# A second gate projected in feature layout in a mixed-attention decoder step: new order of the projection, transposes, and additions moved between engines

## The chip, the cores and the metric

The kernel runs on one core of one Trainium2 chip. The metric is the device time of one execution in microseconds; the time before is the median of three runs. A core has five engines that run side by side and each in its own order: TensorE (PE; its weight loads are listed as PEld), VectorE (DVE), ScalarE (ACT), GpSimd (POOL) and SyncE (SP), which here issues the loads.

## The reference

One layer on 512 prompt tokens and 32 sample tokens, model width 1024: a half-step SwiGLU FFN, a mixing layer, a second half-step FFN, a final RMSNorm. The change is in the mixing layer:

```python
h = rmsnorm(x); z = h @ w_in            # columns: q 512 | k 128 | v 128 | u 512 | gv 512
q, k = rope(q), rope(k)
ya = sliding_window_attention(q, k, v, sinks)          # 8 query heads, 2 key heads, window 128
u  = gelu(z_u)
gv = rmsnorm(gelu(z_gv))                               # over the 512 features of a token
yg = u * (tril(W_s) @ gv + b)                          # per chunk of 128 tokens, 8 heads of 64
x  = x + concat(rmsnorm(ya), rmsnorm(yg)) @ w_out
```

All tensors are float32. The prompt's last chunk of gv and the samples' gv are outputs too.

## The kernel before, in words

All 544 tokens are kept in feature layout: 128 features on the partitions, tokens along the row, x as eight such blocks. A GEMM in full precision is split into three fp32r products: the weight tile and the activation are each held as a high part and a low remainder (wh, wl; xh, xl), and high by high, high by low and low by high are added in PSUM. `gemm_T` (L357) goes over k, and for each k issues six matmuls of 272 columns, three products by two halves of the tokens; after each k it calls `tick`. Weights come by DMA as 128x1024 pieces into four raw buffers; ScalarE makes wh of a piece and VectorE wl (`conv`, L306), one step after each piece of the projection (`conv_step`, L332).

The order of instructions on each engine is fixed at build time by a small planner. `Model` (L41) estimates when each engine is free and when each tile is ready, from a cost for every operation. Work is either main line (the GEMMs, written out in order) or side work: generators that yield a list of what they need (a flag, a tile, a free PSUM slot) ahead of each part. `tick` (L175) is called after each k step: if the estimate of VectorE or ScalarE is more than BACKLOG ahead of TensorE's, it places nothing; otherwise it places the first side work whose needs are met (work marked late only when both are below a third of BACKLOG ahead). `force` (L192) places side work without regard to time until a flag is set.

The mixing layer, `mix` (L821), goes through `Z_ORDER` (L32): k, q0, q1, v, q2, u0, u1, q3, then gv in two halves of 256 columns, then u2, u3. A k, q, v or u piece is 128 output features: one `gemm_T` over 8 k, 48 matmuls, into an accumulator (two buffers `acc`, a third `sp` in places). gv is projected in token layout by `z_gv` (L1233) and `tok_gemm` (L1221): for each half, four tiles of 128 tokens and one of 32, each 8 k by three matmuls with the activation as the stationary operand and 256 columns of weights moving. The result is scaled by the token's 1/rms on its way out of PSUM and lies in `gv` (token on the partition, 512 features along the row).

A q piece is rotated on its way out (`ev_z`, L1172): four ScalarE copies, three VectorE passes, then a split into high and low halves (`split_z`, L1193). Side work meanwhile: `outs` (the k and v outputs), eight attention units (`unit`, L905; four query blocks for each of two head pairs jp), the samples (`samples`, L967), the split and row sums of the attention result (`y_gen`, `a_stat`), and `gmlp` (L1116), late work: gelu and norm of gv, then gelu of u and four times `spatial` (L1092), matmuls named mp and msp. A unit makes scores into the PSUM tile sp (needs the split q and k), exponentials on ScalarE into so, transposes so (tp), and multiplies by v (po) into yT.

The output projection (L1283) has two halves, attention first, each 8 blocks m of 24 matmuls named o. For each m, VectorE multiplies the accumulator by the tokens' 1/rms into a buffer (oa, og) and the buffer is added to x: by GpSimd, except for m = 7 of the gated half. In the gated half `post_norm` (L786) follows: ScalarE makes the new xh and squares, VectorE xl and the running sum ss, from which pss_n and the norm of the second FFN come. The first matmuls of that FFN are named agb and aub.

Of the kernel before, what the change touches and what calls it, by code (L numbers as in the profile page):

```python
# [9 lines left out]
ALU = mybir.AluOpType  # L10
PSUM = bass.MemoryType.PSUM

D = 1024
ND = 8
DFF = 2816
NF = 22
NP = 512
NSMP = 32
NT = NP + NSMP
HT = NT // 2  # L20
# [8 lines left out]

Z_ORDER = (("k", 0), ("q", 0), ("q", 1), ("v", 0), ("q", 2), ("u", 0), ("u", 1), ("q", 3),  # L32
           ("g", 0), ("g", 1), ("u", 2), ("u", 3))
RAW_BUFS = 4
W_BUFS = 5
NX = 14
SLACK = 4500.0
BACKLOG = 3500.0


class Model:  # L41


    def __init__(self):
        self.t = dict(PE=0.0, DVE=0.0, ACT=0.0, POOL=0.0, DMA=1500.0)
        self.log = {}
        self.slot = {}
        self.table = None

    def box(self, ap):  # L50
        (ps, pn), *rest = ap.ap
# [10 lines left out]
        return max((e[4] for e in self.log.get(key, ())), default=0.0)  # L62

    def put(self, eng, ns, reads, writes, lat=100.0):
        reads, writes = [self.box(r) for r in reads], [self.box(w) for w in writes]
        t = max([self.t[eng]] + [self.when(r, True, eng) for r in reads] + [self.when(w, False, eng) for w in writes])
        self.t[eng] = t + ns - {"DVE": 85.0, "ACT": 95.0}.get(eng, 0.0)
        for bs, w in ((reads, False), (writes, True)):
            for key, *b in bs:
                old = self.log.get(key, [])  # L70
                if w:
                    old = [e for e in old if not (b[0] <= e[0] and e[1] <= b[1] and b[2] <= e[2] and e[3] <= b[3])]
                self.log[key] = old[-60:] + [(*b, t + ns + lat, w, eng)]
# [66 lines left out]
class Prog:  # L140
# [16 lines left out]
    def ready(self, g, forced=False):  # L157
        t = self.m.t["PE"]
        for n in g[1]:
            if isinstance(n, tuple):  # L160
                if n not in self.flags:
                    return False
            elif callable(n):
                if not n():
                    return False
            elif forced:
                continue
            elif isinstance(n, str):
                if self.m.free(n) > t:
                    return False  # L170
            elif self.m.when(self.m.box(n)) > t:
                return False
        return True

# [270 lines left out]
    @staticmethod  # L445
    def g2(ap):
        return ap.rearrange("p (g n) -> p g n", g=2)
# [373 lines left out]
    def mix(self, pc, hold):  # L821
        nc = self.nc
        tc = self.tc
        a = self.a
        mm = nc.tensor.matmul
        g2 = self.g2
# [3 lines left out]
        with tc.tile_pool(name="mx", bufs=1) as pm, tc.tile_pool(name="mxr", bufs=2) as pr, scratch:  # L830
# [10 lines left out]
            yT = qT  # L841
# [9 lines left out]
            vt = pm.tile([128, 4, 128], F32, name="vt")  # L851
            vs = pm.tile([32, 128], F32, name="vs")
            gv = pm.tile([128, 5, 512], F32, name="gv")
            u = pm.tile([128, 4, NT], F32, name="u")
            ssa = self.p_st.tile([128, NT], F32, tag="ss", bufs=1, name="ssa")

# [22 lines left out]
            S = self.flags  # L879
# [25 lines left out]
            def unit(i, n, jp):  # L905
# [11 lines left out]
                for g in range(2):  # L917
                    for jj in range(2):
                        o = sp[:, g, jj * 256:jj * 256 + w]
# [13 lines left out]
                v = lambda t: t.rearrange("p (g j) -> p g j", g=2)  # L933
# [10 lines left out]
                PT = [t544(f"PT{i}_{kb}")[:, 0:512] for kb in range(nkb)]  # L944
                for kb in range(nkb):
                    if kb:
                        yield ["po"]
                    tp = self.psum(self.p_ms, ("tr", "po")[kb], f"tp{i}_{kb}")
# [3 lines left out]
                S["so", i] = 1  # L952
                if i == len(UNITS) - 1:
                    S["exp",] = 1
                yield [*PT, "tr", ("v", 0), vt]
                po = self.psum(self.p_ms, "tr", f"po{i}")
                for kb in range(nkb):
                    for g in range(2):
# [8 lines left out]
            def samples():  # L967
                qsv = qs.rearrange("p g b j t -> p g b (j t)")
                yield [qs, "sp"]
                t = pr.tile([128, 576], F32, tag="sT", bufs=1, name="sT")  # L970
# [28 lines left out]
                tp = self.psum(self.p_ms, "po", "tps")  # L999
# [4 lines left out]
                nc.vector.tensor_copy(t[0:32, 256:512], tp[0:32, 256:512])  # L1004
                for g in range(2):
                    gs = slice(g * 64, g * 64 + 64)
                    yield [t, "po", vs]
                    po = self.psum(self.p_ms, "po", f"pos{g}")
                    mm(po[gs, 0:128], vs[:, gs], t[0:32, 256 + g * 128:384 + g * 128], start=True, stop=False)
                    for b in range(8):  # L1010
                        mm(po[gs, b * 16:(b + 1) * 16], vc[:, b, gs], t[:, g * 128 + b * 16:g * 128 + (b + 1) * 16],
                           start=False, stop=(b == 7))
                    nc.vector.tensor_copy(yT[gs, :, NP:NT].rearrange("p j (b t) -> p j b t", b=8),
                                          po[gs, 0:128].rearrange("p (b j t) -> p j b t", b=8, j=4))
# [57 lines left out]
            def a_stat(t0, t1):  # L1072
                yield from self.rstat(ssa, 512, "a", hold_a, t0=t0, t1=t1, parts=2)
# [144 lines left out]
                if (kind, j) == ("v", 0):  # L1218
                    self.flush(hold)

            def tok_gemm(out, s, p):  # L1221
                t0, tn = s * 128, (128 if s < 4 else 32)
                for k in range(ND):
                    wh, wl = self.w[p + k // 4]
                    ws = slice((k % 4) * 256, (k % 4) * 256 + 256)
                    oo = out[:tn, 0, 0:256]
                    xh, xl = self.xh[:, k, t0:t0 + tn], self.xl[:, k, t0:t0 + tn]
                    mm(oo, xh, wh[:, ws], start=(k == 0), stop=False)
                    mm(oo, xh, wl[:, ws], start=False, stop=False)
                    mm(oo, xl, wh[:, ws], start=False, stop=(k == ND - 1))  # L1230
                    self.tick()

            def z_gv(gh):  # L1233
                nonlocal pc
                rs = hold["rs"]
                for s in range(5):
                    ac = self.acc(f"zg{gh}{s}")
                    tok_gemm(ac, s, pc)
                    tn, col = (128, rs[:, s:s + 1]) if s < 4 else (32, rs[0:32, 5:6])
                    o = gv[:tn, s, gh * 256:(gh + 1) * 256]  # L1240
                    self.scale(o, ac[:tn, 0, 0:256], col)
                self.conv_step()
                self.conv_step()
                pc += 2
                S["ng"] = S.get("ng", 0) + 1
                if S["ng"] == 2:
                    S["gv",] = 1

            def z_u(j):
                nonlocal pc  # L1250
                ac = self.acc(f"zu{j}")
                self.gemm_T(ac, pc, 0, self.rh, self.rl, range(ND))
                pc += 1
                nc.vector.tensor_tensor(g2(u[:, j, :]), ac[:, :, :HT], g2(hold["R"]), op=ALU.mult)
                self.conv_step()
                S["nu"] = S.get("nu", 0) + 1
                if S["nu"] == 4:
                    S["u",] = 1
# [2 lines left out]
            self.add_side(outs(), ("v",))  # L1261
            self.add_side(a_stat(384, NT), ("nsplit",))
            self.add_side(a_stat(0, 384), ("ys", 0, 0), ("ys", 1, 0))
            self.add_side(samples(), ("q", 3))
            for i, (n, jp) in enumerate(UNITS):
                self.add_side(unit(i, n, jp), ("q", 2 * jp + 1), ("so", i - 2))
# [4 lines left out]
            for kind, j in Z_ORDER:  # L1271
                if kind == "g":
                    self.flush(hold)
                    z_gv(j)
                elif kind == "u":
                    z_u(j)
                else:
                    z_qk(kind, j, S.get("nz", -1) < 2)
# [4 lines left out]
            for half in range(2):  # L1283
                yo = 8 if half == 0 else 4
                for m in range(ND):
# [4 lines left out]
                    if half == 0 and m < 3:  # L1290
# [7 lines left out]
                        ac = early[m]  # L1298
                    else:
                        ac = self.acc(f"o{half}{m}", True)  # L1300
# [11 lines left out]
                    def ev_g(m=m, ac=ac):  # L1312
                        xm = self.x[:, m, :]
                        if m == 0:
                            S["ss2"] = self.p_st.tile([128, NT], F32, tag="ss", bufs=1, name="ss2")
                            S["post"] = self.post_norm(self.cols[:, 16:24], S["ss2"], "n3")
                        t = t544(f"og{m}")
                        nc.vector.tensor_tensor(g2(t), ac[:, :, :HT], g2(hold_g["R"]), op=ALU.mult)
                        (nc.vector if m == 7 else nc.gpsimd).tensor_tensor(xm, xm, t, op=ALU.add)
                        dead(f"og{m}")  # L1320
                        S["post"](m)

# [202 lines left out]
def _arrange(i):  # L1525
# [5 lines left out]
    for l in (1, 2):  # L1531
# [5 lines left out]
        for ci, (f0, nf) in enumerate(CHUNKS[l]):  # L1537
            t = dn[f0:f0 + nf]
# [6 lines left out]
    q, k, v, u, gv = np.split(w, [512, 640, 768, 1280], axis=1)  # L1545
    q = q.reshape(D, 2, 4, 64).transpose(0, 2, 1, 3).reshape(D, 512)
    lay = lambda t, n: t.reshape(ND, 128, n, 2, 128).transpose(2, 1, 3, 0, 4).reshape(n, 128, 2, ND * 128)
    gl = gv.reshape(2, 4, 128, 2, 256).transpose(3, 2, 0, 1, 4).reshape(2, 128, 2, 1024)
    part = dict(k=k, q=q, v=v, u=u)
    rows, pair = [], []  # L1550
    for n, j in Z_ORDER:
        if n == "g":
            rows.append(gl[j:j + 1])
            continue
        pair.append(part[n][:, j * 128:j * 128 + 128])
        if len(pair) == 2:
            rows.append(lay(np.concatenate(pair, axis=1), 1))
            pair = []
# [62 lines left out]
```

## Time and profile before

| | us |
|---|---|
| median of 3 runs | 971.64 (969.87 to 971.93) |
| the profiled execution | 970.15 |
| its span, first to last instruction | 968.4 |
| mean granted TensorE clock | 0.985 of full speed |
| first FFN ends, mixing layer's k piece begins | 383.5 |
| output projection begins | 514.0 |
| last matmul of the output projection | 573.9 |

A profile row of a group or of the timeline gives the operation, its output and its inputs by the program's names, the shapes, and how many; a bracket tells how long the engine stood idle before it and what ended that. The chain of waits is the path followed back from the last instruction; its rows are start, length, what, and how many in a row, so length by count is the spacing of matmuls that keep TensorE busy. The granted clock is the share of full speed that TensorE was given in a stretch. All rows carry L126, the line of the helper through which each instruction is recorded.

### The profile page before, as it was taken

To read this page: it belongs to the slowest core of one execution; us is meant where nothing else is said; L and a number is where in the kernel's file an instruction comes from. 1 tells how busy PE (TensorE), PEld (TensorE's weight loads), DVE (VectorE), ACT (ScalarE), POOL (GpSimd) and SP (SyncE) were. 2 spreads that over 40 slices of the span, in tenths; PEclk is the share of its full clock that TensorE was granted. 3 is DMA by queue.
4 is the path that set the end of the run, shared out by engine and by line. 5 is a ranking of instruction groups with operands and counts; after the bars stand their busy time and mean duration, and the time that the engine had idled before them with its cause. 6 is when DMAs were issued, how large, how long until landed. Compare 5 with 4: busy or idle time off the path is not lost.

```text
span 968.4 us, 18114 instructions
## 1 busy us (share of the span) xinstructions
PE 945.7 (98%) x7491; PEld 934.2 (96%) x7491; DVE 729.9 (75%) x1309; ACT 412.4 (43%) x656; POOL 57.4 (6%) x62
## 2 busy tenths in 40 slices
PE   8999999999999999999999999999999999999996
PEld 8999999999999999988888989999999999999996
DVE  6789996688668957567676694889985799845864
ACT  7434542245234445555574253334442344512432
POOL 0000000000000000030011640000000000000002
PEclk9999999999999999989999998999999999999998
DMA  7421334222422245112121312203242232512202
GB/s 248 132 66 56 106 90 143 88 87 75 144 71 84 74 148 201 62 56 86 49 85 53 97 62 81 94 30 113 89 142 85 73 99 93 173 46 87 81 9 93
DMA packets 29827, 90.88 MB, mean 94 GB/s; under 512 B 3808, under 2 KB 7248, under 8 KB 29600
## 3 DMA queue, kind: packets, MB, share of 16 engines
q1 hardware_dynamic: 28416, 87.85, 27.8%
q0 software_dynamic: 784, 1.30, 0.4%
q8 instruction: 59, 0.97, 0.4%
q10 hardware_dynamic: 544, 0.56, 0.2%
q14 instruction: 24, 0.20, 0.1%
HBM read 86.98 MB, written 3.74 MB: 94 GB/s over the span
## 4 chain that ended last, share of the span: by engine, by line
PE 90%; DVE 4%; ACT 3%; issue 1%; DMA 1%; SPq 0%; POOL 0%; DVEq 0%; ACTq 0%
PE ada L126 14%; PE adb L126 13%; PE o L126 4%; PE aub L126 3%; PE zu L126 3%; PE zg L126 3%; PE agb L126 2%; PE aga L126 2%; PE aua L126 2%; DVE ss L126 1%; PE zq L126 1%; PE pb_40P L126 1%; PE pa_121P L126 1%; PE pa_40P L126 1%; PE pb_161P L126 1%
## 5 line engine op out<-in xcount | busy, mean ns | idle before, releaser
L126 ACT ACTIVATE wh<-raw 128x1024 fp32r<-128x1024 f32 (+2 forms) x240 | 219.7, 940 | 274.1 <-DVE raw L126 154.5
L126 DVE TENSOR_TENSOR wl<-raw,wh 128x1024 fp32r<-128x1024 f32 (+2 forms) x240 | 256.2, 1079 | 12.6 <-ACT wh L126 12.2
L126 PE MATMUL adb<-hhb,wh 128*128 128x272 f32 x352 | 78.5, 289 | 0.7 <-DVE hpb L126 0.7
L126 PE MATMUL adb<-hlb,wh 128*128 128x272 f32 x352 | 78.0, 288 | 0.9 <-DVE hlb L126 0.9
L126 PE MATMUL adb<-hhb,wl 128*128 128x272 f32 x352 | 77.9, 288 | 0.0
L126 DVE TENSOR_TENSOR raw<-raw,raw 128x512 f32<-128x512 f32 x108 | 74.0, 686 | 1.3
L126 PE MATMUL ada<-hha,wh 128*128 128x272 f32 x352 | 72.9, 288 | 0.9 <-ACT wh L126 0.9
L126 PE MATMUL ada<-hla,wh 128*128 128x272 f32 x352 | 72.7, 288 | 0.0
L126 PE MATMUL ada<-hha,wl 128*128 128x272 f32 x352 | 72.6, 287 | 0.0
L126 DVE SCALAR_TENSOR_TENSOR x<-adb,x 128x272 f32<-128x272 f32 x64 | 25.8, 435 | 47.0 <-PE adb L126 46.9
L126 PEld LDWEIGHTS adb<-hlb,wh 128*128 128x128 f32 x352 | 57.3, 188 | 1.2 <-DVE hlb L126 1.2
L126 PEld LDWEIGHTS adb<-hhb,wh 128*128 128x128 f32 x352 | 57.3, 188 | 0.9 <-DVE hpb L126 0.9
L126 DVE SCALAR_TENSOR_TENSOR x<-ada,x 128x272 f32<-128x272 f32 x64 | 25.1, 433 | 42.6 <-PE ada L126 42.6
L126 PEld LDWEIGHTS adb<-hhb,wl 128*128 128x128 f32 x352 | 57.1, 188 | 0.0
L126 PEld LDWEIGHTS ada<-hha,wh 128*128 128x128 f32 x352 | 55.1, 188 | 1.1 <-issue 1.1
L126 PEld LDWEIGHTS ada<-hla,wh 128*128 128x128 f32 x352 | 55.3, 188 | 0.0
L126 PEld LDWEIGHTS ada<-hha,wl 128*128 128x128 f32 x352 | 55.1, 188 | 0.0
L126 ACT ACTIVATE xh<-x,cols 128x544 fp32r<-128x544 f32 x24 | 17.7, 746 | 36.4 <-DVE x L126 18.0
L126 ACT ACTIVATE hhb<-hpb 128x544 fp32r<-128x544 f32 (+1 forms) x24 | 14.8, 621 | 40.0 <-DVE hpb L126 40.0
L126 PE MATMUL o<-xh,wh 128*128 128x272 f32 x128 | 29.3, 295 | 2.2 <-DVE oa L126 2.2
L126 ACT ACTIVATE hha<-hpa 128x544 fp32r<-128x544 f32 x22 | 14.5, 659 | 39.3 <-DVE hpa L126 39.3
L126 PE MATMUL o<-xh,wl 128*128 128x272 f32 x128 | 28.9, 293 | 0.0
(813 smaller groups left out, 2873.9 us busy)
## 6 DMA issues: line engine op xcount, KB each, us to landing
raw<-wgu SPq DMA_DIRECT2D x86, 512.0 KB, 3.9
raw<-wd SPq DMA_DIRECT2D x32, 384.0 KB, 3.3
raw<-wd SPq DMA_DIRECT2D x20, 512.0 KB, 4.6
raw<-win SPq DMA_DIRECT2D x14, 512.0 KB, 4.3
raw<-wout SPq DMA_DIRECT2D x8, 512.0 KB, 3.7
x<-x SPq DMA_DIRECT2D x8, 272.0 KB, 4.9
y<-x SPq DMA_DIRECT2D x6, 272.0 KB, 2.4
raw<-wgu SPq DMA_DIRECT2D x8, 128.0 KB, 3.6
```

The lines of the kernel that those rows point to most:

```text
L126: return f(*args, **kw)
```

## The change

- `Z_ORDER` becomes k, q0, q1, v, g0, q2, g1, q3, g2, g3, u0 to u3. gv is now four pieces of 128 features, each a `gemm_T` like u, and its weights are laid out as the others are.
- A gv piece is copied out unscaled into free rows of other tensors: g0 and g1 into the places of u2 and u3, g2 and g3 into yT's blocks 2 and 3. New side work, `turn_gv`, waits for all four, transposes them on TensorE, four blocks of 128x128 for each token tile, into the PSUM slots po and tr, and scales by 1/rms on the way into `gv`, whose layout stays.
- What overwrites those places waits for the flag gv: the units of jp = 1 and the samples before they write yT, u2 and u3 before they are evicted.
- In the gated half of the output projection all additions to x are VectorE's.
- The planner: BACKLOG 3500 to 2500; a VectorE operation that reads two SBUF operands is taken to start after a GpSimd operation in flight; a margin, set to zero.

```diff
-Z_ORDER = (("k", 0), ("q", 0), ("q", 1), ("v", 0), ("q", 2), ("u", 0), ("u", 1), ("q", 3),
-           ("g", 0), ("g", 1), ("u", 2), ("u", 3))
+Z_ORDER = (("k", 0), ("q", 0), ("q", 1), ("v", 0), ("g", 0), ("q", 2), ("g", 1), ("q", 3), ("g", 2), ("g", 3), ("u", 0), ("u", 1), ("u", 2), ("u", 3))
...
-BACKLOG = 3500.0
+BACKLOG = 2500.0
+MARGIN = 0.0
...
     def put(self, eng, ns, reads, writes, lat=100.0):
+        two = [r for r in reads if len(r.ap) > 1 and r.ap[-1][1] > 1]
...
+        if eng == "DVE" and sum(r.space != PSUM for r in two) == 2 and self.pool[0] <= t < self.pool[1]:
+            t = self.pool[1]
+        if eng == "POOL":
+            self.pool = (t, t + ns)
...
-            elif self.m.when(self.m.box(n)) > t:
+            elif self.m.when(self.m.box(n)) > t - MARGIN:
...
+            gT = lambda j: u[:, 2 + j, :] if j < 2 else yT[:, j, :]
...
-                yield [*PT, "tr", ("v", 0), vt]
+                yield [*PT, "tr", ("v", 0), vt, ("gv",) if jp else ("v", 0)]
...
-                    yield [t, "po", vs]
+                    yield [t, "po", vs, ("gv",)]
...
-            def z_gv(gh):
+            def z_g(j):
                 nonlocal pc
...
+                ac = self.acc(f"zg{j}")
+                self.gemm_T(ac, pc, 0, self.rh, self.rl, range(ND))
+                pc += 1
+                self.scale(g2(gT(j)), ac[:, :, :HT])
+                self.conv_step()
+                S["ng"] = S.get("ng", 0) + 1
+                if S["ng"] == 4:
+                    S["gT",] = 1
+
+            def turn_gv():
+
+                rs = hold["rs"]
                 for s in range(5):
...
+                    t0, tn, col = (s * 128, 128, rs[:, s:s + 1]) if s < 4 else (NP, 32, rs[0:32, 5:6])
+                    slot = ("po", "tr")[s % 2]
+                    yield [*(gT(j)[:, t0:t0 + tn] for j in range(4)), slot]
+                    tp = self.psum(self.p_ms, slot, f"tg{s}")
+                    for j in range(4):
+                        nc.tensor.transpose(tp[:tn, j * 128:(j + 1) * 128], gT(j)[:, t0:t0 + tn], self.ident)
+                    self.scale(gv[:tn, s, :], tp[:tn, :], col)
+                S["gv",] = 1
...
+                if j >= 2:
+                    self.force(lambda: ("gv",) in S)
                 nc.vector.tensor_tensor(g2(u[:, j, :]), ac[:, :, :HT], g2(hold["R"]), op=ALU.mult)
...
+            self.add_side(turn_gv(), ("gT",))
             self.add_side(samples(), ("q", 3))
...
-                        (nc.vector if m == 7 else nc.gpsimd).tensor_tensor(xm, xm, t, op=ALU.add)
+                        nc.vector.tensor_tensor(xm, xm, t, op=ALU.add)
```

More of the change, by code (lines that the diff above doesn't have):

```diff
@@ L48, in __init__ @@
         self.table = None
+        self.pool = (0.0, 0.0)
     def box(self, ap):
@@ L1219, in z_qk @@
                     self.flush(hold)
[L1221 to L1231, printed above, removed]
-            def z_gv(gh):
-                nonlocal pc
+            def z_g(j):
+                nonlocal pc
+                ac = self.acc(f"zg{j}")
[7 more added lines that the diff above has]
+            def turn_gv():
                 rs = hold["rs"]
                 for s in range(5):
[L1237 to L1247, printed above, removed]
+                    t0, tn, col = (s * 128, 128, rs[:, s:s + 1]) if s < 4 else (NP, 32, rs[0:32, 5:6])
[6 more added lines that the diff above has]
+                S["gv",] = 1
             def z_u(j):
@@ L1273, in mix @@
                     self.flush(hold)
-                    z_gv(j)
+                    z_g(j)
                 elif kind == "u":
@@ L1547, in _arrange @@
     lay = lambda t, n: t.reshape(ND, 128, n, 2, 128).transpose(2, 1, 3, 0, 4).reshape(n, 128, 2, ND * 128)
-    gl = gv.reshape(2, 4, 128, 2, 256).transpose(3, 2, 0, 1, 4).reshape(2, 128, 2, 1024)
-    part = dict(k=k, q=q, v=v, u=u)
+    part = dict(k=k, q=q, v=v, u=u, g=gv)
     rows, pair = [], []
     for n, j in Z_ORDER:
-        if n == "g":
-            rows.append(gl[j:j + 1])
-            continue
         pair.append(part[n][:, j * 128:j * 128 + 128])
```

## The prediction

> **What bounds the kernel now.** I read the page first, then who TensorE waited for, then the stretches of the stage between the two FFNs, then the chain of that stage, and last its timeline where TensorE stood still.
>
> The page:
>
> ```profile
> span 968.4 us, 18114 instructions
> PE 945.7 (98%) x7491; PEld 934.2 (96%) x7491; DVE 729.9 (75%) x1309; ACT 412.4 (43%) x656; POOL 57.4 (6%) x62
> ```
>
> TensorE is the bound: 98% busy, VectorE 75%. What can move the time is the number of matmuls, their spacing, and the few places where PE waits. Those places, from the waits of PE over the whole run (line waited for: us in total, times, longest):
>
> ```profile
> PE pss_n L126 <- DVE ss L126: 2.6, 1, 2.6
> PE o L126 <- DVE oa L126: 2.2, 1, 2.2
> PE sp L126 <- DVE xh L126: 1.8, 1, 1.8
> PE zg L126 <- ACT gv L126: 1.1, 1, 1.1
> PE zg L126 <- DVE zc L126: 0.3, 1, 0.3
> PE sp L126 <- DVE xl L126: 0.3, 1, 0.3
> ```
>
> All six lie in the mixing stage, which is what the change edits. The stretches of that stage and of the FFN behind it (length; busy us and instructions of PE, PEld, DVE, ACT, POOL; granted clock; DMA share; GB/s):
>
> ```profile
> 412.00:421.00 9.00, 7.32 (x33) 6.79 (x34) 7.13 (x22) 4.88 (x7) 0.63 (x2) 0.62 0.36 116
> 421.00:450.00 29.00, 29.00 (x233) 27.80 (x233) 16.98 (x55) 17.12 (x44) 8.46 (x17) 1.00 0.19 62
> 450.00:455.00 5.00, 3.60 (x28) 3.23 (x28) 4.21 (x8) 2.77 (x4) 0.00 (x0) 1.00 0.00 0
> 455.00:514.00 59.00, 59.00 (x492) 53.67 (x493) 42.50 (x148) 34.27 (x100) 4.12 (x7) 1.00 0.22 73
> 553.00:581.00 28.00, 25.67 (x205) 25.45 (x204) 26.13 (x27) 14.06 (x20) 12.70 (x8) 1.00 0.23 76
> 581.00:590.00 9.00, 8.73 (x47) 8.73 (x48) 3.88 (x5) 1.35 (x2) 2.10 (x1) 0.62 0.40 132
> 590.00:700.00 110.00, 109.31 (x872) 109.08 (x871) 91.86 (x152) 45.66 (x65) 0.00 (x0) 1.00 0.24 76
> ```
>
> Two things are to be seen. A gap costs more than its idle time: behind the sp gap the clock is 0.62, and 33 matmuls run in 9 us where 421 to 450 has 233 in 29 (8.0 per us); 33 would take 4.1 us, so 4.9 us are lost for 2.1 us of waiting. And behind the stage PE runs without a gap (109.3 of 110 us), so a microsecond that the stage gains reaches the end.
>
> **The change part by part.** The rows that carry the prices, from the chain of waits of the stage (start, us, what):
>
> ```profile
> 424.18 12.03 PE zu L126 x96
> 438.46 0.44 PE tp L126 x4
> 470.60 5.59 PE zg L126 x48
> 484.68 0.58 PE po L126 x4
> 501.56 1.01 PE po L126 x8
> 514.00 4.17 PE o L126 x33
> 518.17 1.02 PE mp L126 x16
> 529.60 2.66 PE o L126 x12
> 532.26 1.67 PE mp L126 x16
> 540.38 1.01 PE pss_g L126 x10
> 581.27 2.25 PE pss_n L126 x10
> 583.52 2.93 PE agb L126 x12
> 586.45 2.32 PE aub L126 x12
> ```
>
> *gv in feature layout.* Removed: 2 halves x 5 token tiles x 8 k x 3 = 240 matmuls of 256 columns, 5.59/48 = 0.1165 us apart: 28.0 us. The 32-sample tile paid as much as a full one. Added: 4 blocks x 48 = 192 matmuls of the kind of zu, 12.03/96 = 0.1253 us apart: 24.1 us. Added too: 5 x 4 transposes like tp, 0.44 us per four: 2.2 us. Net **-1.7 us** of dense TensorE time.
>
> Evictions, from the timeline:
>
> ```profile
> 454.29 0.47 ACT L126 ACTIVATE gv<-zg,rs_n 128x256 f32<-128x256 f32 x1
> 495.42 0.68 DVE L126 COPY PT<-tp 128x512 f32<-128x512 f32 x1
> ```
>
> Ten reads of the first kind go (4.7 us); four copies of 544 and five scaled copies of 512 columns, near the second, come (6.1 us). They lie beside PE; VectorE is busy 42.5 of 59 us and ScalarE 34.3 in that stretch, so I cost them at nothing; uncovered they would cost 1.4 us. Weight loads keep number and size, one conversion step per piece; only their order changes on SP's queue. MARGIN is zero and does nothing.
>
> *Added waits.* The turn needs all four gT blocks; units 4 to 7 and the samples may write yT only after it, u2 and u3 may be evicted only after it. No instruction waits on an engine queue for this: the planner holds the side work and PE goes on with the GEMM. Unit 4's product came at 484.7. In the new order q3 is still the eighth piece, done before 450 as now; g2 and g3 follow (12 us, some 20 with side work and the turn itself), so gv is there near 470 and the wait is slack. If it were late, units 4 to 7 would shift: the slower rival below.
>
> *q and gv alternate.* Before, zg tiles followed q3 at once and needed the accumulator that q3's long eviction (four ScalarE copies, then three VectorE passes) held: the waits on zc and gv, 1.4 us. Now a whole 6 us GEMM (g2) on another accumulator lies between q3 and g3. Late next would be g2's own eviction, which u0 needs another 6 us later. **-1.4 us.**
>
> *BACKLOG 2500.* The sp gap: unit 0's scores went into the queue when the halves of q1 weren't split. Its rows on the timeline:
>
> ```profile
> 413.31 2.00 ACT L126 ACTIVATE wh<-raw 128x1024 fp32r<-128x1024 f32 x2
> 413.42 0.33 PE L126 MATMUL sp<-KH,xh 128*128 128x128 f32 x1 [1.76 <-DVE xh L126]
> ```
>
> ScalarE had work up to 415.3. The pieces up to v are unchanged, so the scores are again first in line, but the bound that holds them back is 1.0 us lower: one k step (six matmuls, 0.75 us) later, perhaps two. That takes 0.75 to 1.5 us off the 2.1 idle. Whether the clock then falls is open: waits of 1.1 and 0.3 us within 5 us (450 to 455) left it at 1.00, 1.8 and 0.3 did not. So -0.6 (still falls) to -4.9 (gone); I take **-2.2**, one step and an even chance for the clock.
>
> *Additions on VectorE.* Rows of the timeline at the end of the gated half:
>
> ```profile
> 571.62 1.83 POOL L126 TENSOR_TENSOR x<-x,og 128x544 f32<-128x544 f32 x1 [2.43 <-DVE og L126]
> 572.16 1.88 DVE L126 TENSOR_TENSOR ss<-ss,sq_n 128x544 f32<-128x544 f32 x1
> 573.75 0.41 PE L126 MATMUL o<-xh,wl 128*128 128x272 f32 x2
> 577.08 0.71 DVE L126 TENSOR_TENSOR og<-o,R_g 128x544 f32<-128x544 f32 x1
> 577.83 0.73 DVE L126 TENSOR_TENSOR x<-x,og 128x544 f32<-128x544 f32 x1
> 578.47 0.78 DVE L126 SCALAR_TENSOR_TENSOR xl<-x,cols,xh 128x544 fp32r<-128x544 f32 x1
> 579.16 0.72 DVE L126 TENSOR_TENSOR ss<-ss,sq_n 128x544 f32<-128x544 f32 x1
> ```
>
> The same addition into ss takes 1.88 us while GpSimd's addition runs (it ends 0.6 us after that one's end, 573.45) and 0.72 us when GpSimd is idle. So six GpSimd additions each cost VectorE 1.16 us. The last o matmul ends near 574.0, VectorE comes to its og 3.1 us later, and pss_n runs at 581.27. Changed, each block loses 1.16 us and gains 0.73. VectorE's work for a block is then og 0.71, x 0.73, xl 0.78, ss 0.72, and every second block a weight conversion of 1.2: 3.5 us, some 3.3 with starts overlapping, against 24 matmuls or 3.0 us. It falls behind by 0.3 a block, at most 2 us by the last, 1.1 by following the blocks one by one with their idle time. From there og, x, xl, ss, xl, ss take 4.1 us: ss is ready 5.2 us after the last o matmul, not 7.2. TensorE has 48 agb matmuls (6.0 us) for that time, so its wait goes from 2.6 to between 0 and 0.7. With it goes the slow clock: pss_n 2.25 where pss_g took 1.01, twelve agb 2.93 and twelve aub 2.32 where twelve take 1.50, 3.5 us in all. The gap is worth 6.1; I take **-5.5**.
>
> *The wait of o on oa* (2.2 us, then 2.66 for 1.50 and 1.67 for 1.02: 4.0) hangs on where the planner puts the spatial products (mp), whose VectorE work stands ahead of oa. Earlier gv and the lower bound shift it, I can't say which way: 0 to -4.0, once more +2; I take **0**. What the planner now knows of GpSimd moves only its estimates; the gated half has no GpSimd work left to be wrong about.
>
> Sum: -1.7 - 1.4 - 2.2 - 5.5 = **-10.8 us**. The profiled execution took 970.15 us (span 968.4, 1.75 around it): 959.4. It lies 1.5 below the median of 971.64, from which the sum gives 960.8. I say 960.
>
> Two rules of the Trainium skill speak to this. TensorE: Matmul & The Clock Gate, "Why this matters for your kernels", puts the drop of the clock at idle gaps over about 3 us. The traces here differ: 1.8 to 2.6 us of waiting were enough. By that page gaps would cost their idle time alone, and the sum would be about -6.5 (an estimate), 963.7; the measured rows decide. The other is in the rivals.
>
> **The rivals.**
>
> 1. *The output projection waits for attention (slower).* The last split of y, on the timeline:
>
> ```profile
> 503.46 0.65 DVE L126 SCALAR_TENSOR_TENSOR xl<-qT,cols,xh 128x128 fp32r<-128x128 f32 x2 [0.16 <-ACT xh L126]
> ```
>
> The last po ended at 502.6, this at 504.1; o began at 514.0, so 9.9 us of slack. The forecast moves o forward by 5.3, leaving 4.6. For it: side work is placed between k steps, 0.75 us apart instead of 0.36 in the zg tiles, and the lower bound holds it back longer. Against: units 0 to 3 no longer stand behind two u blocks without side work (the 12.03 us of zu in one piece), and VectorE had 16 of 59 us idle. Each microsecond past 4.6 is a microsecond of PE, and a gap adds some 3 us of slow clock. The result is slower than before once the last po comes 13 us later than now (8.4 of waiting and the clock against 10.8 saved): at 16 us later, 974. In smaller doses it gives 962 to 969.
>
> 2. *VectorE becomes the bound of the gated half.* It was busy 26.1 of 28 us there and gets seven additions, 5.1 us. If ss isn't GpSimd's doing, or xl and og slow down, pss_n waits as before and -5.5 falls to 0: 965. Against it stands 0.72 beside 1.88.
>
> 3. *The o wait goes as well:* 956, with the sp gap gone too 953.
>
> 4. *The turn lets the clock fall.* Transposes would have to count as idleness for the clock; five groups in a row are 2.2 us, as long as the o wait, whose slow stretch cost 1.8, that of pss_n 3.5: 962 to 963. Against: 455 to 514 holds transposes four at a time at clock 1.00, and the planner puts one group between two k steps. The skill's same page, "Part 4: PE-mode transpose", says that transposes don't count as busy the same way. The trace agrees with no harm from four; longer runs it doesn't show.
>
> 5. *The change doesn't do what it says:* the scores of unit 0 go out as early as before and new waits elsewhere eat what the shorter GEMM and the alternation save, and only the additions count: 964 to 965.
>
> **How the numbers follow.** Forecast 0.48; rival 1 in its mild form 0.10, without gain 0.06, slower 0.10; rival 2 0.08; rival 3 0.11; rival 4 0.03; rival 5 0.04. What this kernel's measurement can tell from no change is 0.2%, 1.9 us. Faster 0.84, same 0.06, slower 0.10. The forecast's own range is 957 to 964 (the sp gap's ends, 1.4 for evictions). The range to hold 8 in 10 takes in rivals 2, 4, 5, the mild form of 1, and most of 3: 955 to 968.
>
> **What would show it.** 192 zg matmuls like those of zu and 20 new transposes without a clock below 1.00 around them; no PE wait on zc or gv; a shorter wait of sp; ss at 0.72 throughout the gated half, POOL idle there, pss_n about 5 us behind the last o matmul and no clock of 0.62 behind it. Wrong: pss_n still waits over 1.5 us; o's first matmul waits for xh or xl of the attention half; a new gap over 1.5 us among g2 to u3.

## The result, and the profile after

The changed kernel took 961.28 us (median of 8 runs) where the kernel before took 971.43 in the same rounds (median of 8, one of which took 5209 us): ratio 0.9906 with an interval of 0.9890 to 0.9922, so 9.1 us less (7.6 to 10.7). The profiled execution took 960.90. The forecast was 960.0.

The page and the waits of PE in the mixing layer, after:

```profile
span 959.2 us, 18038 instructions
...
PE 939.2 (98%) x7463; PEld 927.1 (97%) x7463; DVE 731.0 (76%) x1316; ACT 412.0 (43%) x655; POOL 46.0 (5%) x55
```

```profile
PE agb L132 <- DVE xl L132: 1.2, 2, 0.9
PE sp L132 <- DVE xh L132: 1.0, 1, 1.0
PE tpv L132 <- DVE vT L132: 0.9, 1, 0.9
PE o L132 <- DVE oa L132: 0.6, 1, 0.6
PE sp L132 <- DVE xl L132: 0.3, 1, 0.3
PE tg L132 <- DVE gv L132: 0.2, 1, 0.2
PE sps L132 <- ACT sT L132: 0.2, 1, 0.2
```

8.3 us of waiting became 4.4. The waits of zg and pss_n are gone, those of sp and o shorter; agb and tpv wait anew. The stretches around the two places with a slow clock (columns as in the prediction):

```profile
410.00:415.00 5.00, 4.37 (x36) 4.22 (x34) 3.10 (x5) 2.77 (x5) 0.00 (x0) 1.00 0.32 105
415.00:420.00 5.00, 3.52 (x20) 3.16 (x21) 4.87 (x12) 3.52 (x4) 0.00 (x0) 0.80 0.23 66
420.00:425.00 5.00, 5.00 (x37) 4.88 (x37) 3.55 (x21) 1.75 (x9) 2.69 (x6) 0.86 0.50 162
570.00:575.00 5.00, 4.13 (x33) 3.91 (x33) 4.93 (x8) 2.40 (x4) 0.00 (x0) 1.00 0.03 11
575.00:580.00 5.00, 4.69 (x39) 4.47 (x38) 5.00 (x7) 2.21 (x3) 1.04 (x1) 1.00 0.22 63
580.00:585.00 5.00, 5.00 (x43) 5.00 (x42) 0.73 (x2) 0.93 (x3) 1.03 (x1) 1.00 0.75 250
```

At the sp gap the clock still falls, for less long; at the end of the output projection it no longer falls. The first and last starts of four groups (columns: shortest, median, longest ns; first to last start):

```profile
L132 PE MATMUL zq<-xh,wl x64: 282/288/292, 393.1 to 448.6; 128*128 128x272 f32 x64
...
L132 PE MATMUL tg<-ident,qT x10: 272/273/273, 476.0 to 481.3; 128*128 128x128 f32 x8, 128*32 128x128 f32 x2
...
L132 PE MATMUL po<-PT,vt x56: 378/380/432, 431.3 to 509.8; 128*64 128x256 f32 x56
...
L132 PE MATMUL o<-xh,wh x128: 283/288/395, 507.8 to 568.2; 128*128 128x272 f32 x128
```

gv is turned only at 481.3, and the last product of an attention unit (po) comes 2.0 us after the output projection has begun. Before, it came 11.6 us ahead.

The layer's first matmul (zk) started at 383.3 before and at 385.2 after, though the instructions ahead of it are the same; over all the traces below it lies between 382.1 and 386.6. So the stages are compared from that start on. Each row is one trace: q3's last matmul, gv ready (last matmul of the turn, or of zg where gv is projected by tokens), the units' last po, the first and last matmul of o, from the last o to the end of the span, and the sum of the last two columns. A row is a single execution, and each fall of the clock in it is worth 1.7 us or a multiple (last section), so differences of that size between rows can be chance. Ratios are from the rounds.

| kernel | ratio (interval) | q3 | gv | last po | o first | o last | rest | all |
|---|---|---|---|---|---|---|---|---|
| before | 1 | 61.7 | 112.9 | 118.9 | 130.5 | 190.6 | 394.5 | 585.1 |
| changed | 0.9906 (0.9890–0.9922) | 63.4 | 96.1 | 124.6 | 122.6 | 183.5 | 390.5 | 574.0 |
| 1 changed, additions back | 0.9935 (0.9914–0.9956) | 64.6 | 97.3 | 125.7 | 123.8 | 184.7 | 393.0 | 577.7 |
| 2 before, additions alone | 0.9928 (0.9907–0.9949) | 60.6 | 111.8 | 117.8 | 129.4 | 188.2 | 389.0 | 577.2 |
| 3 changed, BACKLOG back | 0.9878 (0.9861–0.9896) | 64.8 | 93.1 | 119.2 | 124.8 | 182.5 | 390.4 | 572.9 |
| 4 changed, old order | 1.0018 (0.9998–1.0038) | 61.6 | 107.7 | 135.0 | 131.5 | 197.9 | 389.9 | 587.8 |
| 5 before, layout and order | 0.9905 (0.9881–0.9929) | 65.3 | 93.5 | 119.6 | 125.2 | 182.8 | 391.4 | 574.2 |
| 6 before, BACKLOG alone | 0.9959 (0.9945–0.9974) | 61.9 | 114.2 | 121.2 | 130.6 | 187.6 | 394.1 | 581.7 |
| 7 changed, turn done twice | 0.9909 (0.9893–0.9925) | 63.6 | 99.6 | 128.0 | 126.1 | 187.0 | 390.6 | 577.6 |
| 8 as 3, late scores | 0.9965 (0.9948–0.9982) | 60.4 | 84.4 | 125.9 | 123.0 | 193.5 | 389.7 | 583.2 |
| 9 changed, two bounds | 0.9859 (0.9844–0.9875) | 64.1 | 92.4 | 119.1 | 124.7 | 182.4 | 390.3 | 572.7 |
| 10 before, order alone | 1.0035 (1.0016–1.0055) | 83.5 | 77.5 | 133.8 | 130.6 | 192.9 | 393.4 | 586.3 |
| 11 before, layout alone | 1.0001 (0.9981–1.0021) | 62.5 | 106.4 | 133.0 | 129.8 | 192.0 | 393.1 | 585.1 |
| 12 changed, planner blind | 0.9902 (0.9889–0.9915) | 63.4 | 96.1 | 124.6 | 122.6 | 183.9 | 390.6 | 574.5 |

From before to after the 11.1 us of the trace lie in two places: 7.1 up to the last o matmul, 4.0 behind it. By kind, 3.9 are less waiting and 6.8 less time lost to a slow clock (8.5 before, 1.7 after).

### The profile page after: what moved, and what is told of

The parts are those of the page before. It is cut to its first block, busy times and chain, and to the rows that moved or that the text cites. A ratio compares the mean times of both kernels' runs of the same rounds, so it can differ in the third digit from the quotient of the medians.

```text
span 959.2 us, 18038 instructions
## 1 busy us (share of the span) xinstructions
PE 939.2 (98%) x7463; PEld 927.1 (97%) x7463; DVE 731.0 (76%) x1316; ACT 412.0 (43%) x655; POOL 46.0 (5%) x55
## 4 chain that ended last, share of the span: by engine, by line
PE 89%; DVE 5%; ACT 3%; DMA 1%; issue 1%; SPq 0%; POOL 0%; DVEq 0%
PE ada L132 14%; PE adb L132 14%; PE o L132 3%; PE aub L132 3%; PE zu L132 2%; PE agb L132 2%; PE aga L132 2%; PE zg L132 2%; PE aua L132 2%; PE zq L132 1%; DMA x<-x 1%; PE pb_40P L132 1%; PE pa_121P L132 1%; PE pb_161P L132 1%; PE pa_40P L132 1%; PE pa_61P L132 1%
## 5 line engine op out<-in xcount | busy, mean ns | idle before, releaser
L132 PE MATMUL o<-xl,wh 128*128 128x272 f32 x128 | 28.5, 289 | 0.1
## 6 DMA issues: line engine op xcount, KB each, us to landing
raw<-wgu SPq DMA_DIRECT2D x8, 128.0 KB, 3.7
```

What stands on the lines that cost most here:

```text
L132: return f(*args, **kw)
```

## The experiments

The first theory was the forecast's sum: four separate savings that add up. Its rival: the parts act on one thing, when VectorE and the attention units are done, and so don't add.

**1 and 2: the gated additions, taken back, and alone in the kernel before.**

```diff
-                        nc.vector.tensor_tensor(xm, xm, t, op=ALU.add)
+                        (nc.vector if m == 7 else nc.gpsimd).tensor_tensor(xm, xm, t, op=ALU.add)
```

(the same lines the other way round in 2)

> The changed kernel with the gated half's additions on GpSimd again (961.3 us with them on VectorE, 971.4 before). Theory, the prediction's term: the additions are worth 4 to 5.5 us, so 965 to 967; ss takes 1.8 us beside GpSimd's addition, pss_n runs some 10 us behind the last o matmul and the clock falls behind it. Rival, VectorE is the bound of that half with or without them: within 1 us of 961, clock 1.00 behind the half.

> The kernel before with the additions alone moved to VectorE. Theory: the same term by itself, 4 to 5.5 us off 971.4, so 966 to 967.5, and the wait of pss_n under 1 us, since VectorE enters the half without a backlog here. Rival, the gain at the end needs the other edits: within 1.5 us of 971.4.

Alone they bring 7.0 us (5.0 to 9.0): 963.70. The rest behind o is 389.0 instead of 394.5, 5.5 us less, and ss is ready 5.4 us behind the last o matmul. PE has no gap there, in the stretches of kernel 2:

```profile
570.00:575.00 5.00, 5.00 (x42) 5.00 (x41) 4.96 (x8) 3.21 (x5) 0.00 (x0) 1.00 0.00 0
575.00:580.00 5.00, 5.00 (x42) 4.86 (x42) 4.38 (x6) 1.41 (x2) 2.10 (x1) 1.00 0.34 113
```

In the changed kernel they are worth only 0.0029 of the ratio, 2.8 us (0.2 to 5.4, the two intervals' half-widths taken together as the root of their squares; so below too), and 2.5 us of the trace (393.0 to 390.5). With GpSimd back, PE waits on its timeline for 0.7 us at the first agb and then for 2.7 us in three pieces, and the clock stays at 1.00:

```profile
570.21 0.49 PE L132 MATMUL agb<-xh,wh 128*128 128x272 f32 x2 [0.67 <-DVE og L132]
...
575.93 0.52 PE L132 MATMUL agb<-xh,wh 128*128 128x272 f32 x2 [0.98 <-ACT xh L132]
577.82 0.52 PE L132 MATMUL agb<-xl,wh 128*128 128x272 f32 x2 [1.38 <-DVE xl L132]
...
579.15 0.52 PE L132 MATMUL agb<-xl,wh 128*128 128x272 f32 x2 [0.32 <-DVE xl L132]
```

```profile
575.00:580.00 5.00, 2.38 (x14) 1.94 (x15) 4.96 (x8) 3.84 (x6) 0.10 (x1) 1.00 0.00 0
580.00:585.00 5.00, 5.00 (x44) 5.00 (x43) 3.21 (x4) 0.77 (x1) 2.09 (x1) 1.00 0.48 153
```

So the 3.5 us of slow clock that the forecast credits to the additions are gone in this kernel without them. It isn't the order alone that does it: kernels 10 and 11 below, with GpSimd's additions and only the order or only the layout changed, have the same split waits at agb and no slow clock there.

**3 and 6: the bound, taken back, and alone in the kernel before.**

```diff
-BACKLOG = 2500.0
+BACKLOG = 3500.0
```

(the other way round in 6)

> The changed kernel with BACKLOG 3500 again. Theory: only the sp gap comes back, 1.3 us: 962 to 963, sp waits 2.0 us again. Rival, the bound sets where the side work around the output projection falls: 964 or more with a wait of o of 2 us, or 960 or less if the lower bound holds the side work back.

> The kernel before with BACKLOG 2500 alone. Theory, the prediction's term: the sp gap shrinks by one k step, 0.8 to 2.2 us off 970.6, so 968.5 to 970. Rival, from the run with 3500 in the changed kernel: the lower bound holds the units back, and o or its eviction waits: 971 to 973.

Taken back, the kernel is faster: 959.47, ratio 0.9878, 0.0028 or 2.7 us below the changed kernel (0.4 to 5.0). In the groups of kernel 3 the turn ends 3.0 us earlier behind zk and the last po 5.4, now ahead of o's start, and PE no longer waits for oa.

```profile
L132 PE MATMUL tg<-ident,qT x10: 272/272/273, 472.7 to 477.9; 128*128 128x128 f32 x8, 128*32 128x128 f32 x2
...
L132 PE MATMUL po<-PT,vt x56: 379/379/431, 431.1 to 504.0; 128*64 128x256 f32 x56
...
L132 PE MATMUL o<-xh,wh x128: 283/288/394, 509.6 to 566.8; 128*128 128x272 f32 x128
```

Alone in the kernel before the lower bound brings 4.0 us (2.5 to 5.3): there the units had 11.6 us to spare. Nothing of it comes from the sp gap, for the last q matmul is at 61.9 behind zk instead of 61.7; o takes 57.0 us instead of 60.1, because its wait for oa fell from 2.2 to 0.6 us. The bound also splits the wait of pss_n, but does not remove the slow clock behind it (stretches of kernel 6):

```profile
580.00:585.00 5.00, 3.81 (x21) 3.58 (x22) 4.21 (x6) 1.69 (x3) 1.18 (x1) 0.75 0.21 59
585.00:590.00 5.00, 5.00 (x27) 5.00 (x27) 1.23 (x1) 0.75 (x1) 0.92 (x1) 0.57 0.71 234
```

**4, 5, 10 and 11: order and layout.** 4 is the changed kernel with the order of tiles from before (g0 to g3 in the place of the two halves). 5 is the kernel before with the new layout and the new order, without bound, additions and planner; 11 is 5 with the old order. 10 is the kernel before with its two token halves put into the new places; it leaves the weights of q2 and of the second half of gv mixed up, which changes values but no size or count.

```diff
 # 4 and 11
-Z_ORDER = (("k", 0), ("q", 0), ("q", 1), ("v", 0), ("g", 0), ("q", 2), ("g", 1), ("q", 3), ("g", 2), ("g", 3), ("u", 0), ("u", 1), ("u", 2), ("u", 3))
+Z_ORDER = (("k", 0), ("q", 0), ("q", 1), ("v", 0), ("q", 2), ("u", 0), ("u", 1), ("q", 3), ("g", 0), ("g", 1), ("g", 2), ("g", 3), ("u", 2), ("u", 3))
 # 10
+Z_ORDER = (("k", 0), ("q", 0), ("q", 1), ("v", 0), ("g", 0), ("q", 2), ("g", 1), ("q", 3),
+           ("u", 0), ("u", 1), ("u", 2), ("u", 3))
```

> The changed kernel with the projection in the old order (q2, u0, u1, q3, then the four g, then u2, u3). Theory, the prediction's term: the alternation is worth the waits on zc and gv, 1.4 us at most, of which a whole g GEMM on the other accumulator removes most also here: 961 to 963. Rival, the order sets how early the attention units get their places: their last po comes 5 us or more later against the output projection, and the time is 965 or more.

> The kernel before with the new layout of gv and the new order alone: BACKLOG 3500, the gated additions on GpSimd, the planner blind to GpSimd's reads. Theory, the prediction's terms: 1.7 for the layout and 1.4 for the alternation, 3.1 off 970.6, so 967 to 968. Rival, after the run with the old order: the order is worth far more, since the attention units get their places earlier and o starts earlier; the changed kernel less the additions' 4.0 and plus the 1.9 that the higher bound brought gives 963 to 964.

> The kernel before with its gv still projected in token layout, in the two halves it has, and only the order of tiles changed: g0 after v, g1 between q2 and q3, then u0 to u3. Theory A (the order is what the time came from, not the layout: side work finds places earlier when the two long runs of tiles without attention work are broken up, and the layout brings only its 1.7 us): ratio 0.990 to 0.994, 962 to 965.5; the wait of zg on gv may stay, since five token tiles still follow each other. Rival B (the layout is needed, because token tiles give places to side work each with an accumulator and an eviction of its own in the way): ratio 0.996 or above, 967 or more.

> The kernel before with gv in feature layout and the turn on TensorE alone; order of tiles, bound, additions and planner as before. Theory A (in the old order the layout makes gv and with it units 4 to 7 late, as in the fourth experiment, where the last po came after o's start): slower than before by about the fourth experiment's loss with the additions still on GpSimd, ratio 1.000 to 1.008, 971 to 979, o's first matmul behind the last unit or waiting. Rival B (the layout's 1.7 us are gained in either order, and the fourth experiment's loss was due to the lower bound in the old order): ratio 0.995 to 0.999, 966.5 to 970.5.

The old order in the changed kernel gives all of it back: 972.11. PE then waits for the units (waits of kernel 4):

```profile
PE tp L132 <- ACT so L132: 5.1, 1, 5.1
PE mp L132 <- DVE kT L132: 1.8, 1, 1.8
PE o L132 <- DVE oa L132: 1.1, 1, 1.1
```

Layout and order together bring 9.2 us by themselves (6.9 to 11.6): 962.20. Layout alone: 971.62, no difference. Order alone: 973.71, 3.4 us slower (1.6 to 5.3); theory A of that run fell. Why neither does it alone is in the groups of 11 and of 10. Kernel 11:

```profile
L132 PE MATMUL tg<-ident,qT x10: 272/273/273, 486.3 to 491.2; 128*128 128x128 f32 x8, 128*32 128x128 f32 x2
...
L132 PE MATMUL po<-PT,vt x56: 379/380/686, 443.6 to 517.8; 128*64 128x256 f32 x56
...
L132 PE MATMUL o<-xh,wh x128: 283/288/575, 514.6 to 576.3; 128*128 128x272 f32 x128
```

Kernel 10:

```profile
L126 PE MATMUL zq<-xh,wl x64: 283/289/292, 392.4 to 468.0; 128*128 128x272 f32 x64
...
L126 PE MATMUL po<-PT,vt x56: 379/380/431, 428.4 to 518.3; 128*64 128x256 f32 x56
...
L126 PE MATMUL o<-xh,wh x128: 283/288/575, 515.1 to 576.9; 128*128 128x272 f32 x128
```

Units 4 to 7 need q3 and, in the new layout, the turned gv. In 11 q3 comes at 62.5 as before, but the turn ends at 106.4 and the last po 26.6 us later, after o has begun. In 10 the halves of gv, 14 us each, push q3 to 83.5, and the last po is again late. Of the orders tried only the new one, with two short blocks (6 us each) between the q tiles and two behind them, gives both early. In the table the last po comes 26.1 to 28.5 us after the turn in nine of the ten kernels with the new layout (not in 8).

**7: the turn done twice.**

```diff
-                    for j in range(4):
+                    for j in (0, 1, 2, 3, 0, 1, 2, 3):
                         nc.tensor.transpose(tp[:tn, j * 128:(j + 1) * 128], gT(j)[:, t0:t0 + tn], self.ident)
```

> The changed kernel with each transpose of the turn done twice, 20 more into the same places. Theory: 0.11 us each on TensorE's path, 2.2 us in all, 963 to 964, clock 1.00 around the turn, groups of eight in a row. Rival, transposes count as idleness for the clock: 965 or more and a clock below 1.00 there. Third, the turn lies in slack: under 962.

By the rounds 962.87, ratio 0.9909: 0.3 us more than the changed kernel, with an uncertainty of 2.2. In the trace the turn ends 3.5 us later, and last po and o's start 3.4 and 3.5 later. The rounds don't settle whether that shift is paid in full. Of the 3.6 us in the trace (577.6 against 574.0), 1.7 are a fall of the clock at 461, ahead of the turn. For the clock at the turn the stretches of kernel 7 are clear:

```profile
475.00:480.00 5.00, 5.00 (x44) 5.00 (x43) 3.97 (x12) 3.81 (x12) 0.00 (x0) 1.00 0.31 105
480.00:485.00 5.00, 5.00 (x45) 4.89 (x44) 1.49 (x2) 0.97 (x2) 0.00 (x0) 1.00 0.32 105
```

**8: the sp gap closed by placing its work 2 us later** (in kernel 3).

```diff
-                        "sp", ("so", i - 2), ("go", i - 1)]
+                        "sp", ("so", i - 2), ("go", i - 1),
+                       lambda: i or self.m.when(self.m.box(Q[1][:, 8:10, 0:128])) + 2000 <= self.m.t["PE"]]
...
-                yield [vT, "tr"]
+                yield [vT, "tr", lambda: self.m.when(self.m.box(vT)) + 2000 <= self.m.t["PE"]]
```

> The changed kernel with BACKLOG 3500 (959.5 us), and unit 0's scores and the transposes of v placed 2 us later by the planner's clock, so that their operands are there. Theory, the sp gap is worth its idle time and the slow clock behind it: both go, 3 to 5 us, so 955 to 957. Rival, the later start of unit 0 passes on to all units, which end after o has begun, as in the old order: 962 or more.

967.08, ratio 0.9965: 8.4 us above kernel 3 (6.1 to 10.8), though the sp gap and the slow clock behind it are gone. The waits of kernel 8 are those of late units:

```profile
PE o L132 <- DVE xl L132: 2.4, 3, 1.7
PE mp L132 <- DVE kT L132: 1.8, 1, 1.8
PE tp L132 <- DVE so L132: 1.3, 1, 1.3
```

**9 and 12: two bounds, and the planner without GpSimd.**

```diff
 # 9
-BACKLOG = 2500.0
+BACKLOG = 3500.0
...
-        if max(self.m.t["DVE"], self.m.t["ACT"]) > self.m.t["PE"] + BACKLOG:
+        if max(self.m.t["DVE"], self.m.t["ACT"]) > self.m.t["PE"] + (BACKLOG if ("so", 0) in self.flags else 2500.0):
 # 12
-            t = self.pool[1]
+            pass
```

> The changed kernel with the lower bound of 2500 only until unit 0's scores are placed, 3500 from there on. Theory A (the lower bound has two effects: it shortens the gap of sp, which is worth 1.3 us, and it holds the attention units back, which costs about 2.7 us in this kernel; the two can be had apart): the third experiment's time less the gap, some 958 to 959.5, ratio 0.986 to 0.988; sp waits 1.0 and 0.3 as in the changed kernel, the last po ends before o's first matmul as in the third experiment, no wait of o on oa. Rival B (the time of the third experiment came from the sp gap standing where it does, since a later sp pushes every unit back as in the eighth): units late again, 961 or more, ratio 0.989 or above.

> The changed kernel with the planner's estimate no longer delaying VectorE for GpSimd's operations. Theory A (with the additions on VectorE the gated half has no GpSimd work left to be wrong about, and elsewhere the estimate moves nothing that PE waits for): same as the changed kernel within 0.2%, ratio 0.988 to 0.993. Rival B (the estimate decides where the additions or the units' steps are placed, so part of the gain hangs on it): ratio 0.994 or above.

Kernel 9 took 958.2 us (four runs), ratio 0.9859, whose interval lies below that of the changed kernel. From kernel 3 (0.9878) it can't be told apart: 1.8 us less, with an uncertainty of 2.3. Its page and waits:

```profile
span 955.1 us, 18035 instructions
```

```profile
PE agb L132 <- DVE xl L132: 1.1, 2, 0.8
PE sp L132 <- DVE xh L132: 1.0, 1, 1.0
PE tpv L132 <- DVE vT L132: 0.6, 1, 0.6
```

Theory A holds only in part. sp waits 1.0 and the units are early, but behind zk this trace is only 0.2 us shorter than kernel 3's: of the shorter gap 0.7 us is left at the end of zg (84.1 against 84.8) and 0.1 at o's start. Most of the difference to the changed kernel's span, 2.8 of 4.1 us, lies ahead of zk. Kernel 12 took 962.22, ratio 0.9902, the same as the changed kernel within 2.0 us: the planner's knowledge of GpSimd shows no worth here.

## Why the prediction was right, and which of its terms were not

The total was right: 960.0 against 961.28, and faster. The sum was not right term by term; three errors cancelled, and that the total came out so near is luck. From kernel 5 to 3 to the changed one the rounds split it: layout and order -9.2 (uncertain by 2.3), additions (with the planner, which shows no worth) -2.6 (by 2.9), the bound +2.7 (by 2.3). The forecast had -3.1, -5.5 and -2.2.

*Layout and alternation (forecast -1.7 and -1.4).* 192 zg matmuls at a median of 288 ns like the other projections, 20 transposes, no wait on zc or gv: as said; the clock is below 1.00 only in g0, where the sp gap now falls. Up to o's start the trace of kernel 5 gained 5.3 us, where 3.1 were forecast. Part of it is side work that now runs behind o's start (14 small matmuls, pss_a and rb_a), and 1.7 is that the clock stayed down half as long behind the same sp gap, which the edit doesn't explain. The rest of the 9.2 came from terms that the forecast held apart: the wait of o on oa is gone in 5 (o takes 57.6 us instead of 60.1), for which 0 was taken, and the single wait of pss_n with its slow clock is gone too (391.4 instead of 394.5). The step that failed was to price the order by the two waits it removes; it also moves the later work of VectorE, and with it the waits on oa and ss. That kernels 4, 10 and 11, whose units end over 3 us after o's start (2.0 in the changed kernel), lose all of the gain fits this; why the wait of pss_n goes in 10 and 11 too is open.

*"The wait is slack".* The flag gv was forecast near 470; the turn ended at 481.3, for the first transposes started at 475.8, 6.5 us behind the last zg. Unit 4's product came at 488.2 (484.7 before), and units 4 to 7 then end some 28 us after the turn. The slack of o was forecast to shrink by 5.3 us; counted from the last po it shrank by 13.6, from 11.6 to -2.0. That is rival 1 in its mild form, and at o's start it cost nothing: o's first matmuls waited for nothing, and one wait of 0.6 us for oa was left. Kernels 4, 8, 10 and 11 show what it costs when the units are later.

*BACKLOG (forecast -2.2).* Its mechanism at the sp gap was right: one k step later, a wait of 1.0 instead of 1.8. On the timeline after:

```profile
415.37 0.33 PE L132 MATMUL sp<-KH,xh 128*128 128x128 f32 x1 [1.00 <-DVE xh L132]
...
416.29 0.33 PE L132 MATMUL sp<-KH,xl 128*128 128x128 f32 x1 [0.26 <-DVE xl L132]
...
418.39 1.11 PE L132 MATMUL tpv<-ident,vT 128*128 128x128 f32 x4 [0.86 <-DVE vT L132]
```

The clock fell again, and tpv waits anew, so the shorter wait brought nothing that can be seen. The worth of the bound in the kernel before, 4.0 us, lies mostly in the wait of o on oa and the slow clock behind it (o is 3.1 of the 3.4 us that the trace gained), which the forecast took at 0; in the new order kernel 5 has no such wait left to remove. There the bound costs 2.7 us (0.4 to 5.0). It holds back every later piece of side work, which the forecast names only for rival 1, and the units end after o's start; but behind zk the two traces differ by only 1.1 us (574.0 and 572.9), so that the late units are the price is argued, not shown.

*Additions (forecast -5.5).* By the trace exactly that in the kernel before (394.5 to 389.0); by the rounds 7.0 (5.0 to 9.0). In the changed kernel ss takes 0.72 throughout, GpSimd idle, and no slow clock follows; but VectorE enters the gated half late, on the timeline after:

```profile
552.91 0.72 DVE L132 TENSOR_TENSOR og<-o,R_g 128x544 f32<-128x544 f32 x1 [3.23 <-ACT R_g L132]
...
569.03 0.72 DVE L132 TENSOR_TENSOR ss<-ss,sq_n 128x544 f32<-128x544 f32 x1
...
575.81 0.72 DVE L132 TENSOR_TENSOR ss<-ss,sq_n 128x544 f32<-128x544 f32 x1
```

It waits for the gated norm, whose spatial products (mp) began at 141.3 instead of 134.8 behind zk. ss is ready 7.8 us after the last o matmul (568.7), not 5.2, and PE pays 0.9 and 0.3 us at agb. The price was right for the kernel before and not for this one: 3.5 of the 5.5 us were slow clock, which the other edits remove too, so the two can't both be credited.

*Rivals 2 to 5.* Rival 2 didn't come, since pss_n doesn't wait; but VectorE is busy throughout the end of the gated half and PE waits for it 1.2 us at agb. Rival 3 came in part: most of its o wait, but not the sp gap. Rival 4 didn't come: two turns' worth of transposes leave the clock at 1.00. By the Trainium skill (TensorE: Matmul & The Clock Gate, "Part 4: PE-mode transpose") transposes don't count as busy the same way; in groups of eight between GEMM steps the trace of kernel 7 shows no harm. Rival 5 is refuted by kernel 5.

*The rule on gaps.* The same page of the Trainium skill, TensorE: Matmul & The Clock Gate, "Why this matters for your kernels", would have no drop below about 3 us of idling. The sp gap after, 1.0, 0.3 and 0.9 us, contradicts it; the pieces of 0.98, 1.38 and 0.32 in kernel 1 agree with it.

What stays open is why, in the changed kernel and in 1, 5, 10 and 11, the planner's sequence at the end of o has pss_n behind all of PE's waits instead of in front of the last agb; no run changed that alone.

## What to carry to other kernels

Where side work is placed by a planner, price an edit of the order by when the last of the side work will be done and what needs it, not by the waits it removes: here layout or order alone brought nothing, together 9.2 us. Don't add the worth of edits that each remove the same gap or the same slow clock. When several edits come as one, undo each by itself: one of them (the bound) cost 2.7 us (0.4 to 5.0) of what the others gained. And don't explain a difference of 2 or 3 us between two single traces before it is seen that the clock fell at the same places in both.

## What the runs showed of the hardware

A fall of the clock has a size. Looked at in stretches of 0.5 us, every fall in the first 600 us of these fourteen traces goes down to 0.50 and loses 1.7, 3.4 or 5.1 us (the share missing from 1.00, added up), so it lasts some 3.4, 6.8 or 10.2 us. The length of the waiting alone doesn't say whether it comes; the places that recur in several kernels:

| waits of PE, us | us lost to the clock behind them, by kernel |
|---|---|
| sp 1.8 and 0.3 (then tpv 0.5 to 0.9, but not in the kernel before) | before 3.4; 2, 3 and 5: 1.7; 10: 0; 11: 3.4 |
| sp 1.0 and 0.3, then tpv 0.6 to 0.9 | changed, 7, 9 and 12: 1.7; 1, 4 and 6: 3.4 |
| tpv 0.9 alone | 8: 0 |
| o for oa 2.2 | before 1.7; 2: 0 |
| pss_n 2.6 | before 3.4 |
| agb 1.0, pss_n 1.2 | 6: 3.4 |
| agb 1.0, 1.4 and 0.3 (in 5 the last two) | 1, 5, 10 and 11: 0 |

The kernel before and kernel 2 give PE the same instructions in the same order until pss_n, and yet the clock behind the same wait for oa differs (first line before, second line kernel 2). In kernel 10 it doesn't fall at the sp gap at all (last two lines):

```profile
529.00:534.00 5.00, 4.40 (x32) 3.98 (x32) 2.96 (x5) 0.85 (x1) 4.38 (x3) 0.66 0.34 103
527.00:532.00 5.00, 4.71 (x46) 4.35 (x47) 4.47 (x7) 0.54 (x1) 4.69 (x3) 1.00 0.34 107
...
412.00:417.00 5.00, 2.94 (x23) 2.55 (x21) 4.16 (x8) 3.24 (x4) 0.00 (x0) 1.00 0.15 53
417.00:422.00 5.00, 4.47 (x38) 4.35 (x38) 4.97 (x22) 2.65 (x8) 1.17 (x3) 1.00 0.63 202
```

So a part of each trace's time is chance, and the shorter wait at sp shows no smaller loss than the longer one. In 4, 7 and 10 the clock also fell once with no wait of more than 0.3 us in the 6 us ahead, behind the samples' narrow matmuls (128x16 and 128x32 operands), which run in other traces without a fall; what decides it isn't shown.

The moment of the layer's first matmul varied by 4.5 us between traces with the same instructions up to there, more than several of the effects looked for. That is the clock too: 382.1 and 382.4 where it lost nothing ahead of that matmul (2 and 9), 383.3 to 385.3 where it lost 1.7, and 386.2 to 386.6 where it lost 3.4 (6, 8 and 12).
